# A two-layer encoder kernel: the sums of hT placed after the second pair of heads, and the last pair's norm run beside the last dilated head

## The chip, the cores and the metric

The kernel runs on one core of a Trainium2 chip. The metric is the device time in microseconds (us) of one execution, the median of the runs shown.

## The reference

Two layers of a hybrid encoder on 512 positions of width 1024, everything in float32, and a last RMSNorm. A layer normalises its input, makes all projections with one matrix `w_in`, runs three kinds of attention on them, gates and merges them, and adds an output projection to the input. Cut to what the change is near:

```python
def mixer_layer(x, mem, layer_idx, g_norm, w_in, lam_p, w_mem_kv, g_mem, ...):
    h = rmsnorm(x, g_norm)
    z = jnp.einsum('bsd,dn->bsn', h, w_in)
    dq, dk, dv, dg, lq, lk, lv, lg, mq, mg, mgate = jnp.split(z, splits, axis=-1)
    ...
    o_a = diff_attention(dq, dk, dv, lam, rel_bias[:, :8])      # 8 heads, two softmax maps each
    o_a = rmsnorm(o_a) * (1.0 - lam_init)                       # over the 128 values of a head
    y_a = (o_a * silu(dg)) @ w_br_diff
    ...                                                         # 3 x 4 dilated window heads -> y_b
    ...                                                         # 4 memory heads -> y_m
    gates = jax.nn.sigmoid(mgate).reshape(B, S, 3, D_MODEL)
    merged = gates[:, :, 0] * y_a + gates[:, :, 1] * y_b + gates[:, :, 2] * y_m
    return x + merged @ w_out
```

## The kernel before

**Precision and engines.** Each float32 product is made of three matmuls on halves: a value is split into a rounded `hi` and a rest `lo` (`split`: ACT writes `hi` with a copy, DVE writes `lo` as the difference; L106 and L107), and `mm3` (L214 to L217) issues hi·hi, hi·lo and lo·hi. PE is TensorE, DVE VectorE, ACT ScalarE, POOL GpSimd, SP the engine whose queue issues most DMAs.

**Weights.** They come in one fixed order. SP issues the loads into `w_raw` (three buffers), ACT makes `w_hi` (four buffers) and DVE `w_lo` (three), two weights ahead of the projection that uses them. A projection to feature-major form (`proj_fm`) is 24 matmuls into one of four PSUM buffers with the tag "mm"; `b_ps` and `f_ms`, below, use the same four.

**One layer.** `hT_hi` and `hT_lo` hold the normalised input, transposed. At the start of layer 0 the memory keys and values, the memory queries (`m_qh`, `m_ql`) and the table of relative biases (`bias_tables`: three matmuls `b_ps` and copies `b_t` on DVE, L350 and L352, behind one done ahead) are made. Then come four steps j = 0 to 3, each with one pair of differential heads and one dilated head. `weave` runs generators by turns, so that their code is issued mixed: first `dil_proj(j)` with `diff_att(j)`, then `diff_proj(j+1)` with `dil_att(j)`. In `diff_att` each head makes scores `f_s`, a DVE operation that adds the bias and finds the row minimum (`tensor_tensor_reduce`, L532; its result is `f_e`), an Exp on ACT, the weighted difference of the two maps on DVE, PE transposes (`wT_ps`), their split (`f_wThi`, `f_wTlo`), and the products with the values into `f_o`, which ACT copies to `f_osb`. `dil_att` is alike, with scores `d_s` and exponentials `d_e`. `diff_norm(j)` follows at the end of each step: for each of the two heads a Square on ACT (`f_sq`), its split (`f_sqh`, `f_sql`), two matmuls with ones (`f_ms`), an Identity on ACT, a reciprocal on DVE (L569), and two stores (`u_d`, `v_d`).

**The sums of hT.** Late in the layer, in `merge`, pairs of gate projections are made with fewer products, by sums of quarters of hT. `right_sums` (L256 to L282) makes them as `t_sum`: for each of two halves ten DVE operations and four stores to `t_d`, with four buffers. Its generator is woven into step j = 1. `merge` loads them back with POOL's DMAs (`t_in`).

**What sets the order.** The program is recorded in the order of the code, but the order on each engine is set by a scheduler, which may issue an instruction earlier where its operands and buffers allow; `tc.issue_after(x)` keeps what is recorded under it from being placed ahead of instruction x. Within an engine, and within SP's queue, instructions then run in that order, and one that waits holds all behind it.

Of the kernel before, what the change touches and what calls it, by code (L numbers as in the profile page):

```python
# [9 lines left out]
F32 = mybir.dt.float32  # L10
# [3 lines left out]
ALU = mybir.AluOpType  # L14
# [40 lines left out]
def encoder_kernel(ctx: ExitStack, tc: tile.TileContext, x, mem, g_norm, w_in, diff_lambda,  # L55
# [196 lines left out]
        add(c12, prod(3, 0, b22), c12)  # L252

    H0, H1 = slice(0, 256), slice(256, 512)

    def right_sums(pool):  # L256

        def acc(out, x, y, op):
            nc.vector.tensor_tensor(out=out, in0=x, in1=y, op=op)

        for k2 in range(2):
            def quarter(kh, ts):
                ks = slice(4 * kh + 2 * k2, 4 * kh + 2 * k2 + 2)
                return f32(hT_hi[:, ks, ts]), f32(hT_lo[:, ks, ts])

            b11, b12, b21, b22 = quarter(0, H0), quarter(0, H1), quarter(1, H0), quarter(1, H1)
            t1, t2, t3, t4 = [pool.tile([128, 2, 256], F32, tag="ts", name="t_sum", bufs=4) for _ in range(4)]
            for t, x, y in ((t1, b12, b11), (t3, b22, b12)):
                acc(t, x[0], y[0], ALU.subtract)
                yield  # L270
                acc(t, t, x[1], ALU.add)
                yield
                acc(t, t, y[1], ALU.subtract)
                yield
            for t, x, y in ((t2, b22, t1), (t4, b21, t2)):
                acc(t, x[0], y, ALU.subtract)
                yield
                acc(t, t, x[1], ALU.add)
                yield
            for i, t in enumerate((t1, t2, t3, t4)):  # L280
                dma(t_d[i, k2], t)
            yield  # L282
# [41 lines left out]

    def bias_tables(pool):

        lh = pool.tile([105, 96], F32, tag="tmp", name="b_lh", bufs=3)[:, 0:4 * N_BIAS]
        for i in range(3):
            for r in range(4):
                pdma(lh[35 * i:35 * i + 32, r * N_BIAS:(r + 1) * N_BIAS], rel_bias)  # L330
# [178 lines left out]
    def diff_att(l, j, P, proj, lam):  # L509
        Q, K, vhi, vlo = proj  # L510
        O = []
        for s in range(2):
# [5 lines left out]
            for half in range(2):  # L518
                whi = P["ae"].tile([128, 4, 256], F32R, tag="x4", name="f_wThi", bufs=4)
                wlo = P["ae"].tile([128, 4, 256], F32R, tag="x4", name="f_wTlo", bufs=4)  # L520
                for c2 in range(2):
# [4 lines left out]
                    for m in range(2):  # L526
# [2 lines left out]
                        nc.tensor.matmul(sp, lhsT=qh[:, cs], rhs=K[s, m], start=True, stop=False)  # L529
                        nc.tensor.matmul(sp, lhsT=ql[:, cs], rhs=K[s, m], start=False, stop=True)  # L530
                        em = P["al"].tile([128, S], F32, tag="e", name="f_e", bufs=4)
                        nc.vector.tensor_tensor_reduce(  # L532
                            out=em.rearrange("p (c b) -> p c b", c=4), in0=sp, in1=bt[:, 3 - c:7 - c],
                            op0=ALU.add, op1=ALU.min, scale=-1.0, scalar=3e38, accum_out=stt[:, m:m + 1])
                        nc.scalar.activation(em, em, AF.Exp, scale=-1.0, bias=stt[:, m:m + 1],  # L535
                                             accum_out=stt[:, 2 + m:3 + m])
                        e.append(em)
# [18 lines left out]

    def diff_norm(j, P, O):

        for s, o in enumerate(O):
            tmp = lambda name, dt=F32: P["al"].tile([128, S], dt, tag="tmp", name=name, bufs=3)  # L560
            sq, sqh, sql = tmp("f_sq"), tmp("f_sqh", F32R), tmp("f_sql", F32R)
            nc.scalar.activation(sq, o, AF.Square)
            split(sqh, sql, sq)
            ms = mm([128, S], name="f_ms")
            nc.tensor.matmul(ms, lhsT=ones, rhs=sqh, start=True, stop=False)
            nc.tensor.matmul(ms, lhsT=ones, rhs=sql, start=False, stop=True)
            dma(u_d[2 * j + s], o)
            nc.scalar.activation(sq, ms, AF.Identity, bias=eps_t, scale=1.0 / 128)
            nc.vector.reciprocal(sq, sq)  # L569
            dma(v_d[2 * j + s], sq)  # L570


    def qk_split(ae, o, scale, n0):
# [247 lines left out]
    for l in range(DEPTH):  # L821
# [48 lines left out]
        for j in range(4):  # L870
            dp, O = weave((dil_proj(l, j, P), 10), (diff_att(l, j, P, fp, lam), 8))
            if j < 3:
                gens = [(diff_proj(l, j + 1, P), 8), (dil_att(l, j, P, dp), 4)]
                if j == 1:
                    gens.append((right_sums(al), 22))
                fp = weave(*gens)[0]
            else:
                weave((dil_att(l, j, P, dp), 4))
            diff_norm(j, P, O)
        close(al_c)  # L880
        close(ae_c)
        yu_c, yu = opened(f"yu{l}", "left")
# [86 lines left out]
```

## Time and profile before

| | before |
|---|---|
| median of three runs | 1755.63 us (1754.11 to 1756.03) |
| profiled execution | 1754.84 us |
| its span | 1753.1 us |
| mean granted clock of TensorE in it | 0.997 of 2.4 GHz |
| PE busy | 1724.0 us (98%) |
| DVE, ACT, POOL busy | 1152.4, 888.9, 174.0 us |

The span runs from the first to the last instruction in the profile; 1.7 us of the time lie around it. A share of busy time is over the whole span; where an engine stands idle is read from windows and from the waits. "PE mm L215 <- DVE b_t L352" means that a matmul on line 215 into `mm` stood for the instruction that writes `b_t` on line 352, or for what that one set free.

### The profile page before, as it was taken

The numbers are of one execution on the slowest core, as the hardware profiler recorded it, in microseconds if no ns is written. First come the engines' busy times: TensorE is split into PE (matmuls) and PEld (weight loads), VectorE is DVE, ScalarE is ACT, GpSimd is POOL, SyncE is SP. The second block draws the span as 40 slices with busy tenths as digits, with TensorE's granted clock in tenths as the row PEclk, the third lists the DMA queues.
The fourth block names the chain that finished last, engine by engine and source line by source line (L and its number), as shares of the span: only waits on it lengthen the run. The fifth ranks groups of instructions, "written<-read, shape, count | busy, mean of one in ns | idle before, by whom it ended". The sixth has DMA issues, their size and how long they took to land.

```text
span 1753.1 us, 25712 instructions
## 1 busy us (share of the span) xinstructions
PE 1724.0 (98%) x9732; PEld 1515.8 (86%) x9732; DVE 1152.4 (66%) x1963; ACT 888.9 (51%) x1516; POOL 174.0 (10%) x141
## 2 busy tenths in 40 slices
PE   7899999999999999999999999999999999999998
PEld 6698889889898889998888998898988888889986
DVE  6766575666766586676476756667657647766663
ACT  6355555545545573343354655455455548533433
POOL 2200000000000033341000000000000100344200
PEclk9999999999999999999999999999999999999999
DMA  9752243332443643332663333324323438333242
GB/s 266 170 135 84 77 119 96 93 89 83 114 132 98 204 145 98 102 108 82 203 190 110 108 95 94 88 82 114 102 78 105 136 90 251 105 97 109 85 151 78
DMA packets 313084, 208.80 MB, mean 119 GB/s; under 512 B 15268, under 2 KB 284580, under 8 KB 312960
## 3 DMA queue, kind: packets, MB, share of 16 engines
q1 hardware_dynamic: 309648, 199.28, 39.0%
q0 software_dynamic: 3312, 7.88, 1.9%
q8 instruction: 76, 1.25, 0.3%
q14 instruction: 48, 0.39, 0.1%
HBM read 182.08 MB, written 25.02 MB: 118 GB/s over the span
## 4 chain that ended last, share of the span: by engine, by line
PE 95%; DMA 2%; DVE 1%; ACT 1%; issue 1%; SPq 0%; ACTq 0%; DVEq 0%
PE mm L215 23%; PE mm L217 23%; PE mm L216 23%; PE s_mm L217 4%; PE s_mm L215 4%; PE s_mm L216 4%; PE wT_ps L506 2%; PE f_s L529 2%; PE f_s L530 2%; DMA w_raw<-in_w_mem_kv 1%; PE f_o L216 1%; PE f_o L215 1%; PE f_o L217 1%; PE d_o L655 1%; PE d_s L631 1%
## 5 line engine op out<-in xcount | busy, mean ns | idle before, releaser
L107 DVE TENSOR_TENSOR w_lo<-w_raw,w_hi 128x1024 fp32r<-128x1024 f32 (+2 forms) x256 | 304.7, 1191 | 218.9 <-PE mm L217 171.6
L106 ACT ACTIVATE w_hi<-w_raw 128x1024 fp32r<-128x1024 f32 (+2 forms) x256 | 250.8, 980 | 389.2 <-PE mm L216 197.4
L215 PE MATMUL mm<-hT_hi,w_hi 128*128 128x512 f32 x1024 | 405.7, 397 | 5.1 <-DVE b_t L352 2.8
L217 PE MATMUL mm<-hT_hi,w_lo 128*128 128x512 f32 x1024 | 403.0, 394 | 0.0
L216 PE MATMUL mm<-hT_lo,w_hi 128*128 128x512 f32 x1024 | 403.0, 394 | 0.0
L215 PEld LDWEIGHTS mm<-hT_hi,w_hi 128*128 128x128 f32 x1024 | 193.2, 189 | 45.6 <-DVE b_t L352 4.5
L217 PEld LDWEIGHTS mm<-hT_hi,w_lo 128*128 128x128 f32 x1024 | 193.0, 188 | 39.9
L216 PEld LDWEIGHTS mm<-hT_lo,w_hi 128*128 128x128 f32 x1024 | 193.4, 189 | 38.1 <-DVE hT_lo L107 0.2
L217 PE MATMUL mm<-w_hi,hT_lo 128*128 128x384 f32 (+2 forms) x640 | 210.0, 330 | 0.0
L215 PE MATMUL mm<-w_hi,hT_hi 128*128 128x384 f32 (+2 forms) x640 | 209.6, 328 | 0.0
L216 PE MATMUL mm<-w_lo,hT_hi 128*128 128x384 f32 (+2 forms) x640 | 208.2, 326 | 0.0
L106 ACT ACTIVATE w_hi<-s_raw 128x1024 fp32r<-128x1024 f32 x80 | 76.1, 952 | 168.7 <-PE mm L216 105.1
L215 PEld LDWEIGHTS mm<-w_hi,hT_hi 128*128 128x128 f32 x640 | 120.9, 189 | 6.0
L216 PEld LDWEIGHTS mm<-w_lo,hT_hi 128*128 128x128 f32 x640 | 120.8, 189 | 6.1
L217 PEld LDWEIGHTS mm<-w_hi,hT_lo 128*128 128x128 f32 x640 | 120.7, 189 | 5.1
L107 DVE TENSOR_TENSOR w_lo<-s_raw,w_hi 128x1024 fp32r<-128x1024 f32 x80 | 99.1, 1239 | 32.8 <-issue 32.8
L535 ACT ACTIVATE f_e<-f_e,f_st 128x512 f32<-128x512 f32 x128 | 92.0, 721 | 49.7 <-DVE f_st L532 49.7
L294 POOL DMA_DIRECT2D t_in<-t_d x16 | 8.9, 562 | 1013.1 <-PE f_o L217 582.2
L215 PE MATMUL mm<-u_hi,w_hi 128*128 128x512 f32 x256 | 101.2, 395 | 0.0
L216 PE MATMUL mm<-u_lo,w_hi 128*128 128x512 f32 x256 | 101.2, 395 | 0.0
L217 PE MATMUL mm<-u_hi,w_lo 128*128 128x512 f32 x256 | 101.1, 395 | 0.0
L532 DVE CUSTOM_DVE_ANT_0 f_e<-f_s,f_bias 128x512 f32<-128x512 f32 x128 | 84.4, 682 | 6.8 <-PE f_s L530 6.7
(248 smaller groups left out, 3365.4 us busy)
## 6 DMA issues: line engine op xcount, KB each, us to landing
w_raw<-in_w_in SPq DMA_DIRECT2D x128, 512.0 KB, 4.0
s_raw<-in_w_in SPq DMA_DIRECT2D x80, 256.0 KB, 3.1
w_raw<-in_w_in SPq DMA_DIRECT2D x96, 128.0 KB, 2.4
w_raw<-in_w_mem_kv SPq DMA_DIRECT2D x16, 512.0 KB, 5.9
w_raw<-in_w_in SPq DMA_DIRECT2D x32, 256.0 KB, 2.9
u_raw<-u_d SPq DMA_DIRECT2D x32, 256.0 KB, 4.8
w_raw<-in_w_br_diff SPq DMA_DIRECT2D x16, 512.0 KB, 4.1
w_raw<-in_w_out SPq DMA_DIRECT2D x16, 512.0 KB, 3.8
```

Of the source, the lines that this page charges most:

```text
L106: nc.scalar.activation(hi, src, AF.Copy)
L107: nc.vector.tensor_tensor(out=lo, in0=src, in1=f32(hi), op=ALU.subtract)
L215: nc.tensor.matmul(o, lhsT=lh, rhs=rh, start=start, stop=False)
L216: nc.tensor.matmul(o, lhsT=lh, rhs=rl, start=False, stop=False)
L217: nc.tensor.matmul(o, lhsT=ll, rhs=rh, start=False, stop=stop)
L506: nc.tensor.transpose(t[:, i], s, ident)
L529: nc.tensor.matmul(sp, lhsT=qh[:, cs], rhs=K[s, m], start=True, stop=False)
L530: nc.tensor.matmul(sp, lhsT=ql[:, cs], rhs=K[s, m], start=False, stop=True)
L532: nc.vector.tensor_tensor_reduce(out=em.rearrange("p (c b) -> p c b", c=4), in0=sp, in1=bt[:, 3 - c:7 - c], op0=ALU.add, op1=ALU.min, scal ...
L535: nc.scalar.activation(em, em, AF.Exp, scale=-1.0, bias=stt[:, m:m + 1], accum_out=stt[:, 2 + m:3 + m])
L631: nc.tensor.matmul(sp2[:, g - 1], lhsT=Q[g][:, cs], rhs=K[g][:, cs], start=True, stop=True)
L655: nc.tensor.matmul(oh[:, qs], lhsT=v23[:, c, (g - 1) * 128:g * 128], rhs=w23[:, g - 1, qs], start=False, stop=c2 == 1 and g == 2)
```

## The change

The list `mark` keeps the latest `tensor_tensor_reduce` of `diff_att`. The DVE operations of `right_sums` are recorded under `issue_after` of that instruction; as the generator runs after the second pair's `diff_att`, it is the last reduce of that pair. `diff_norm` becomes a generator in two parts: first Square, split and the store of `u_d` for both heads, then, head by head, the matmuls, the Identity, the reciprocal and the store of `v_d`. For j < 3 it is run to its end in the place where it stood; for j = 3 it is woven with `dil_att`. Its temporary buffers are six instead of three.

```diff
@@ -252,11 +252,13 @@
         add(c12, prod(3, 0, b22), c12)
 
     H0, H1 = slice(0, 256), slice(256, 512)
+    mark = []
 
     def right_sums(pool):
 
         def acc(out, x, y, op):
-            nc.vector.tensor_tensor(out=out, in0=x, in1=y, op=op)
+            with tc.issue_after(mark[0].ins):
+                nc.vector.tensor_tensor(out=out, in0=x, in1=y, op=op)
 
         for k2 in range(2):
             def quarter(kh, ts):
@@ -324,7 +326,7 @@
 
     def bias_tables(pool):
 
-        lh = pool.tile([105, 96], F32, tag="tmp", name="b_lh", bufs=3)[:, 0:4 * N_BIAS]
+        lh = pool.tile([105, 96], F32, tag="tmp", name="b_lh", bufs=6)[:, 0:4 * N_BIAS]
         for i in range(3):
             for r in range(4):
                 pdma(lh[35 * i:35 * i + 32, r * N_BIAS:(r + 1) * N_BIAS], rel_bias)
@@ -529,9 +531,9 @@
                         nc.tensor.matmul(sp, lhsT=qh[:, cs], rhs=K[s, m], start=True, stop=False)
                         nc.tensor.matmul(sp, lhsT=ql[:, cs], rhs=K[s, m], start=False, stop=True)
                         em = P["al"].tile([128, S], F32, tag="e", name="f_e", bufs=4)
-                        nc.vector.tensor_tensor_reduce(
+                        mark[:] = [nc.vector.tensor_tensor_reduce(
                             out=em.rearrange("p (c b) -> p c b", c=4), in0=sp, in1=bt[:, 3 - c:7 - c],
-                            op0=ALU.add, op1=ALU.min, scale=-1.0, scalar=3e38, accum_out=stt[:, m:m + 1])
+                            op0=ALU.add, op1=ALU.min, scale=-1.0, scalar=3e38, accum_out=stt[:, m:m + 1])]
                         nc.scalar.activation(em, em, AF.Exp, scale=-1.0, bias=stt[:, m:m + 1],
                                              accum_out=stt[:, 2 + m:3 + m])
                         e.append(em)
@@ -556,18 +558,23 @@
 
     def diff_norm(j, P, O):
 
+        parts = []
         for s, o in enumerate(O):
-            tmp = lambda name, dt=F32: P["al"].tile([128, S], dt, tag="tmp", name=name, bufs=3)
+            tmp = lambda name, dt=F32: P["al"].tile([128, S], dt, tag="tmp", name=name, bufs=6)
             sq, sqh, sql = tmp("f_sq"), tmp("f_sqh", F32R), tmp("f_sql", F32R)
             nc.scalar.activation(sq, o, AF.Square)
             split(sqh, sql, sq)
+            dma(u_d[2 * j + s], o)
+            parts.append((sq, sqh, sql))
+        yield
+        for s, (sq, sqh, sql) in enumerate(parts):
             ms = mm([128, S], name="f_ms")
             nc.tensor.matmul(ms, lhsT=ones, rhs=sqh, start=True, stop=False)
             nc.tensor.matmul(ms, lhsT=ones, rhs=sql, start=False, stop=True)
-            dma(u_d[2 * j + s], o)
             nc.scalar.activation(sq, ms, AF.Identity, bias=eps_t, scale=1.0 / 128)
             nc.vector.reciprocal(sq, sq)
             dma(v_d[2 * j + s], sq)
+            yield
 
 
     def qk_split(ae, o, scale, n0):
@@ -874,9 +881,10 @@
                 if j == 1:
                     gens.append((right_sums(al), 22))
                 fp = weave(*gens)[0]
+                for _ in diff_norm(j, P, O):
+                    pass
             else:
-                weave((dil_att(l, j, P, dp), 4))
-            diff_norm(j, P, O)
+                weave((dil_att(l, j, P, dp), 4), (diff_norm(j, P, O), 4))
         close(al_c)
         close(ae_c)
         yu_c, yu = opened(f"yu{l}", "left")
```

The lines below are those that the scheduled programs have. Numbers behind a name tell one buffer or tile from another; line numbers shift by up to 7 in the changed kernel.

**DVE at the start of layer 0**, around the last copies of the bias tables, before the change (`w_lo` are weights' low halves, `m_ql` those of the memory queries):

```order
L259 TENSOR_TENSOR t_sum_3280<-t_sum_3280,hT_lo_89 128x512
L107 TENSOR_TENSOR w_lo_555<-w_raw_552,w_hi_554 128x1024
L259 TENSOR_TENSOR t_sum_3282<-t_sum_3282,hT_lo_89 128x512
L580 SCALAR_TENSOR_TENSOR m_ql_549<-mm_523,m_qh_548 128x512
L259 TENSOR_TENSOR t_sum_3280<-t_sum_3280,hT_lo_89 128x512
L107 TENSOR_TENSOR w_lo_590<-w_raw_587,w_hi_589 128x1024
L259 TENSOR_TENSOR t_sum_3282<-t_sum_3282,hT_lo_89 128x512
L580 SCALAR_TENSOR_TENSOR m_ql_584<-mm_558,m_qh_583 128x512
L259 TENSOR_TENSOR t_sum_3281<-hT_hi_88,t_sum_3280 128x512
L259 TENSOR_TENSOR t_sum_3281<-t_sum_3281,hT_lo_89 128x512
L107 TENSOR_TENSOR w_lo_737<-w_raw_734,w_hi_736 128x1024
L352 COPY b_t_661<-b_ps_659 80x512
```

and after it:

```order
L354 COPY b_t_653<-b_ps_651 80x512
L107 TENSOR_TENSOR w_lo_555<-w_raw_552,w_hi_554 128x1024
L587 SCALAR_TENSOR_TENSOR m_ql_549<-mm_523,m_qh_548 128x512
L107 TENSOR_TENSOR w_lo_590<-w_raw_587,w_hi_589 128x1024
L587 SCALAR_TENSOR_TENSOR m_ql_584<-mm_558,m_qh_583 128x512
L107 TENSOR_TENSOR w_lo_737<-w_raw_734,w_hi_736 128x1024
L354 COPY b_t_661<-b_ps_659 80x512
L354 COPY b_t_673<-b_ps_671 80x512
L354 COPY b_t_681<-b_ps_679 80x249
```

The `t_sum` operations are gone from here; `b_t_661` comes right behind `w_lo_737` in both.

**DVE at the end of the second pair of heads in layer 0**, before the change:

```order
L538 RECIPROCAL f_st_2880<-f_st_2880 128x2
L539 TENSOR_TENSOR f_st_2880<-f_st_2880,lam_707 128x1
L540 TENSOR_SCALAR f_e_2890<-f_e_2890,f_st_2880 128x512
L541 SCALAR_TENSOR_TENSOR f_e_2884<-f_e_2884,f_st_2880,f_e_2890 128x512
L107 TENSOR_TENSOR f_wTlo_2823<-wT_ps_2841,f_wThi_2822 128x4x128
L107 TENSOR_TENSOR w_lo_2951<-w_raw_2948,w_hi_2950 128x1024
L107 TENSOR_TENSOR d_vlo_2784<-mm_2786,d_vhi_2783 128x128
L107 TENSOR_TENSOR d_vlo_2784<-mm_2787,d_vhi_2783 128x128
L107 TENSOR_TENSOR d_vlo_2784<-mm_2788,d_vhi_2783 128x128
```

and after it:

```order
L261 TENSOR_TENSOR t_sum_3033<-t_sum_3033,hT_lo_89 128x512
L540 RECIPROCAL f_st_2880<-f_st_2880 128x2
L261 TENSOR_TENSOR t_sum_3035<-t_sum_3035,hT_lo_89 128x512
L261 TENSOR_TENSOR t_sum_3033<-t_sum_3033,hT_lo_89 128x512
L541 TENSOR_TENSOR f_st_2880<-f_st_2880,lam_707 128x1
L261 TENSOR_TENSOR t_sum_3035<-t_sum_3035,hT_lo_89 128x512
L107 TENSOR_TENSOR f_wTlo_2823<-wT_ps_2841,f_wThi_2822 128x4x128
L261 TENSOR_TENSOR t_sum_3034<-hT_hi_88,t_sum_3033 128x512
L542 TENSOR_SCALAR f_e_2890<-f_e_2890,f_st_2880 128x512
L107 TENSOR_TENSOR w_lo_2951<-w_raw_2948,w_hi_2950 128x1024
L261 TENSOR_TENSOR t_sum_3034<-t_sum_3034,hT_lo_89 128x512
L543 SCALAR_TENSOR_TENSOR f_e_2884<-f_e_2884,f_st_2880,f_e_2890 128x512
```

The `t_sum` operations now stand between the steps of the last softmax difference (`f_st`, `f_e`) and ahead of the split `f_wTlo`; the later ones follow behind these rows, mixed with the `d_vlo` splits.

**PE at the last pair of heads in layer 0**, from the last product of the second head, before the change:

```order
L217 MATMUL f_o_4899<-f_wThi_5036,f_vlo_4388 128x256
L215 MATMUL d_s1_5249<-d_kh_4654,d_qh_4725 128x512
L216 MATMUL d_s1_5249<-d_kl_4655,d_qh_4725 128x512
L217 MATMUL d_s1_5249<-d_kh_4654,d_ql_4726 128x512
L565 MATMUL f_ms_5379<-f_sqh_5374,ones_82 128x512
L215 MATMUL mm_5410<-hT_hi_88,w_hi_5134 128x512
```

and after it:

```order
L217 MATMUL f_o_4899<-f_wThi_5036,f_vlo_4388 128x256
L215 MATMUL d_s1_5269<-d_kh_4654,d_qh_4725 128x512
L216 MATMUL d_s1_5269<-d_kl_4655,d_qh_4725 128x512
L217 MATMUL d_s1_5269<-d_kh_4654,d_ql_4726 128x512
L638 MATMUL d_s2_5273<-d_k_4786,d_q_4857 128x128
L638 MATMUL d_s2_5273<-d_k_4892,d_q_4959 128x128
L572 MATMUL f_ms_5308<-f_sqh_5212,ones_82 128x512
L215 MATMUL mm_5410<-hT_hi_88,w_hi_5134 128x512
```

Two score matmuls `d_s2` moved ahead of the matmul of the norm, which keeps its place behind `f_o` and `d_s1`.

**ACT at the same place**, before the change:

```order
L568 ACTIVATE f_sq_5360<-f_ms_5366,eps_t_84 128x512
L605 ACTIVATE d_v23_4999<-mm_5003 128x256
L552 ACTIVATE f_osb_5130<-f_o_4899 128x512
L562 ACTIVATE f_sq_5373<-f_osb_5130 128x512
L106 ACTIVATE f_sqh_5374<-f_sq_5373 128x512
L638 ACTIVATE d_e_5223,d_st_5222<-d_e_5223,d_st_5222 128x768
```

and after it:

```order
L574 ACTIVATE f_sq_5204<-f_ms_5261,eps_t_84 128x512
L612 ACTIVATE d_v23_4999<-mm_5003 128x256
L645 ACTIVATE d_e_5237,d_st_5236<-d_e_5237,d_st_5236 128x768
L554 ACTIVATE f_osb_5130<-f_o_4899 128x512
L565 ACTIVATE f_sq_5211<-f_osb_5130 128x512
L106 ACTIVATE f_sqh_5212<-f_sq_5211 128x512
L645 ACTIVATE d_e_5268,d_st_5267<-d_e_5268,d_st_5267 128x768
```

An Exp (`d_e`) moved ahead of the copy `f_osb` of the second head's result.

## Rows read from the trace of the kernel before

**Rows 1.** the busy table of the page: busy time of each engine, its share of the span, instructions.

```profile
PE 1724.0 (98%) x9732; PEld 1515.8 (86%) x9732; DVE 1152.4 (66%) x1963; ACT 888.9 (51%) x1516; POOL 174.0 (10%) x141
```

**Rows 2.** windows of the span: from:to in us, length, busy us of PE, PEld, DVE, ACT and POOL with their instructions, mean granted TensorE clock (1.00 is 2.4 GHz, 0.50 is 1.2 GHz), DMA share, GB/s.

```profile
50.00:75.00 25.00, 20.97 (x91) 17.00 (x90) 18.85 (x29) 7.76 (x15) 5.37 (x10) 0.92 0.67 166
70.00:75.00 5.00, 3.71 (x10) 2.96 (x11) 5.00 (x9) 2.85 (x9) 3.01 (x6) 0.66 0.91 234
275.00:300.00 25.00, 25.00 (x148) 23.71 (x148) 16.91 (x38) 13.40 (x28) 0.00 (x0) 1.00 0.40 109
300.00:325.00 25.00, 25.00 (x130) 21.51 (x129) 13.43 (x28) 13.25 (x26) 0.00 (x0) 1.00 0.17 53
525.00:550.00 25.00, 23.65 (x124) 20.04 (x123) 18.25 (x29) 15.03 (x28) 0.00 (x0) 1.00 0.38 122
905.00:935.00 30.00, 30.00 (x138) 24.79 (x137) 26.33 (x39) 14.47 (x21) 0.00 (x0) 1.00 0.71 218
1375.00:1400.00 25.00, 23.33 (x133) 20.77 (x133) 15.58 (x30) 11.75 (x23) 4.57 (x8) 1.00 0.53 166
```

**Rows 3.** waits of PE over the whole span: what waited, for what, us in total, times, longest.

```profile
PE mm L215 <- DVE b_t L352: 2.8, 1, 2.8
PE f_ms L565 <- ACT f_sqh L106: 2.6, 2, 1.3
...
PE b_ps L350 <- DVE m_ql L580: 1.2, 1, 1.2
PE f_ms L566 <- DVE f_sql L107: 0.3, 1, 0.3
```

**Rows 4.** timeline of PE, layer 0, 59 to 79 us: start, length, engine, line, operation, out<-in, tile, count, and in brackets the idle time before it and what ended it. From the first row to the second are 23 matmuls, from the fourth to the fifth 24.

```profile
59.76 0.39 PE L216 MATMUL mm<-hT_lo,w_hi 128*128 128x512 f32 x1
...
64.97 0.38 PE L350 MATMUL b_ps<-b_oh,b_parts 105*80 105x512 bf16 x1
...
68.23 0.27 PE L350 MATMUL b_ps<-b_oh,b_parts 105*80 105x249 bf16 x1 [1.24 <-DVE m_ql L580]
71.29 0.80 PE L215 MATMUL mm<-hT_hi,w_hi 128*128 128x512 f32 x1 [2.79 <-DVE b_t L352]
...
78.42 0.39 PE L215 MATMUL mm<-hT_hi,w_hi 128*128 128x512 f32 x1
```

**Rows 5.** timeline of DVE in the same stretch, same columns.

```profile
60.41 0.69 DVE L259 TENSOR_TENSOR t_sum<-hT_hi 128x512 f32<-128x512 f32 x1 [6.05 <-DMA t_d<-t_sum]
61.02 0.68 DVE L259 TENSOR_TENSOR t_sum<-t_sum,hT_lo 128x512 f32<-128x512 f32 x1
...
62.82 1.22 DVE L107 TENSOR_TENSOR w_lo<-w_raw,w_hi 128x1024 fp32r<-128x1024 f32 x1
...
70.56 1.28 DVE L352 COPY b_t<-b_ps 80x512 f32<-80x512 f32 x2
```

**Rows 6.** timeline of SP's queue (first row) and of ACT (second row) in the same stretch.

```profile
51.73 10.32 SPq L281 DMA_DIRECT2D t_d<-t_sum  x4
...
68.15 1.06 ACT L106 ACTIVATE w_hi<-w_raw 128x1024 fp32r<-128x1024 f32 x1 [6.83 <-DMA w_raw<-in_w_in]
```

**Rows 7.** all instructions that write or read the tile `t_sum`: line, engine, operation, count, ns as min/median/max, first and last start; the last row is the time of its stores `t_d<-t_sum` from issue to landing.

```profile
L259 DVE TENSOR_TENSOR t_sum<-t_sum,hT_lo x24: 674/683/693, 49.8 to 930.2; 128x512 f32<-128x512 f32 x24
...
DMA to landing us min/median/max: 2.0/4.3/8.7
```

**Rows 8.** timelines at the last pair of heads: ACT in layer 0 (three rows), PE in layer 0 (one), then PE and DVE in layer 1.

```profile
532.20 0.60 ACT L552 ACTIVATE f_osb<-f_o 128x512 f32<-128x512 f32 x1 [0.70 <-PE f_o L217]
...
533.49 0.63 ACT L106 ACTIVATE f_sqh<-f_sq 128x512 fp32r<-128x512 f32 x1
534.96 0.94 ACT L638 ACTIVATE d_e<-d_e,d_st 128x768 f32<-128x768 f32 x1 [0.83 <-DVE d_st L635]
...
534.18 0.50 PE L565 MATMUL f_ms<-f_sqh,ones 128*128 128x512 f32 x1 [1.32 <-ACT f_sqh L106]
...
1399.69 0.51 PE L566 MATMUL f_ms<-f_sql,ones 128*128 128x512 f32 x1 [0.32 <-DVE f_sql L107]
...
1398.94 0.69 DVE L107 TENSOR_TENSOR f_sql<-f_sq,f_sqh 128x512 fp32r<-128x512 f32 x1 [4.24 <-DMA v_d<-f_sq]
```

**Rows 9.** timelines at the second pair of heads, layer 0: DVE (first row), PE (the rest).

```profile
304.17 0.68 DVE L107 TENSOR_TENSOR f_wTlo<-wT_ps,f_wThi 128x512 fp32r<-128x512 f32 x1
...
302.04 0.60 PE L506 MATMUL wT_ps<-ident,f_e 128*128 128x128 f32 x4
...
304.05 0.48 PE L215 MATMUL mm<-hT_hi,w_hi 128*128 128x512 f32 x1
...
309.08 0.28 PE L216 MATMUL f_o<-f_wTlo,f_vhi 128*128 128x256 f32 x1
```

**Rows 10.** timelines at the first pair of heads, layer 0: DVE (two rows), PE (last row).

```profile
238.00 3.35 DVE L569 RECIPROCAL f_sq<-f_sq 128x512 f32<-128x512 f32 x1
...
242.86 0.73 DVE L541 SCALAR_TENSOR_TENSOR f_e<-f_e,f_st 128x512 f32<-128x512 f32 x1
...
248.49 0.49 PE L506 MATMUL wT_ps<-ident,f_e 128*128 128x128 f32 x3
```


## The prediction, on record before the changed kernel was run

> **What bounds the kernel now.** I read the busy table first, then the windows, then PE's waits, then single instructions. PE is busy 1724.0 of 1753.1 us [rows 1], so 29.1 us is everything a pure reordering can win from its idle time; the work itself is unchanged by the diff (the same matmuls, the same vector passes). The windows say where those 29 us lie. Some 22 us lie at the start and end, where the change moves nothing. Three places are left that it touches: 50 to 75 us, where 25.00 − 20.97 = 4.03 us are idle and the granted clock is 0.92; 525 to 550 us, 1.35 us idle; 1375 to 1400 us, 1.67 us idle [rows 2]. PE's waits give each a name [rows 3]: 2.8 us for the bias tables' copy `b_t` and 1.2 us for `m_ql` (the first place), twice 1.3 us for ACT's `f_sqh` and 0.3 us for DVE's `f_sql` (the other two: the norm of the last two heads, once a layer).
>
> **First place: why PE waits for a DVE copy.** The mixing of work there is seen on DVE [rows 5]: a `t_sum` stood 6.05 us for a store `t_d<-t_sum`, and everything behind it on DVE waited with it. On SP four such stores sit from 51.73 to 62.05, because each waits for its sum, and the weight loads behind them on that queue come late too: ACT's `w_hi` waited 6.83 us for `w_raw` and began at 68.15 [rows 6]. `w_lo` of that weight and behind it the two copies `b_t` (70.56, in program order after it) are what PE's next projection waits for: its PSUM buffer is held by the first `b_ps`. So PE stands 1.24 us at 68.23 and 2.79 us before 71.29, in sum 4.03 [rows 4].
>
> The wait has a second price. After it the windows show a granted clock of 0.66 in 70 to 75 us [rows 2], so part of that stretch ran at 1.2 GHz instead of 2.4. The next projection's 24 matmuls took 78.42 − 71.29 = 7.13 us; at the pace before the stall, (64.97 − 59.76)/23 = 0.2265 us each, they take 5.44 [rows 4]. The clock cost 1.69 us. Whole price of the place: 5.7 us.
>
> **What the change does to it.** The twenty `t_sum` operations of a layer can't start before the last reduce of the second pair of heads, so in layer 0 they leave this stretch of DVE altogether, and their eight stores leave SP's queue. What follows on DVE in the new order is `w_lo`, `m_ql`, `w_lo`, `m_ql`, then `w_lo_737`, then `b_t_661`. By hand, with the durations of before: the load for weight 737 is no longer behind a blocked store; `w_lo_737` then waits only for a weight buffer that PE gives back when the projection that ended at 64.97 is through, takes 1.22 us [rows 5] and ends at about 66.2; `b_t_661` adds 0.64 (half of the 1.28 of two copies [rows 5]): 66.8. PE finishes the memory scores at 68.23 − 1.24 = 66.99 and reaches the projection at about 67.1 with the third `b_ps` (0.27, [rows 4]) before it. The copy is there some 0.3 us ahead, so I expect no wait and no fall of the clock: −5.7 us. The margin is thin and makes a rival below.
>
> Here a page bears on the size. The Trainium skill, "TensorE: Matmul & The Clock Gate", section "What's actually happening", says that the number of slow matmuls after a restart changes from run to run of one kernel (6, 11, 14). This trace has one case only, 7 to 8 slow starts. By the page and the step of 0.43 instead of 0.23 us the clock's share could be an estimated 1.2 to 2.8 us rather than 1.69, and the saving 5.2 to 6.8.
>
> **Where the twenty sums go.** They stand behind the reduces of the second pair, in layer 0 from about 295 us, in layer 1 from about 1152. One takes 0.68 us [rows 7], 0.61 from start to start (60.41 to 61.02 [rows 5]), so 12 us are put into a stretch in which DVE has 25 − 16.91 = 8.1 us free in 275 to 300 and 11.6 free in 300 to 325 [rows 2]. Fourteen of them stand ahead of the `f_wTlo` that ran at 304.17 [rows 9]; walked through with the waits of before it ends at about 309.5 instead of 304.85. Who waits for it is PE's `f_o` matmul at 309.08 [rows 9], which in the new PE order stands behind the whole projection and part of the next: 42 matmuls after 304.05 at 0.2275, that is 313.7. The slack is about 4 us. Before that PE wants `f_e` for the transposes that ran at 302.04; the new DVE order gives it at about 302.2 and PE comes to them at 303.7: slack 1.5. In layer 1 the kernel before already had these sums elsewhere (907 to 931 us), with a `t_d` store among the weight loads in the same way, and PE was busy 30.00 of 30.00 us in 905 to 935 [rows 2]. I take nothing for the move. Its bounds: a gain is excluded, since PE has no idle time in 275 to 325; a loss has its price among the rivals.
>
> **The last pair.** The chain on ACT is `f_osb` at 532.20, then Square, then `f_sqh` at 533.49, and `f_ms` starts at 534.18: 1.98 us of three dependent ACT steps after `f_o`. PE had 0.66 us of `d_s` to put between, and stood for 1.32 [rows 8]. The new code is meant to mix the norm of both heads into the last dilated head, but the second head's sum of squares can't begin before its `f_o` is complete, and in the new order PE still has just `f_o`, three `d_s1`, now two `d_s2` (pulled ahead, about 0.3 us), then `f_ms`. On ACT an Exp of 0.94 us now stands ahead of `f_osb`, where in before it came after the chain [rows 8]; by hand the chain starts 0.15 us later in layer 0 and 0.3 later in layer 1. So the wait shrinks by the 0.3 of `d_s2` and grows by 0.15 to 0.3: I take −0.1 in the first and 0 in the second. The third wait, 0.32 us at 1399.69, is another matter: `f_sql` there stood 4.24 us for a store of `f_sq`, that is for one of three temporary buffers [rows 8]. With six it has no such wait: −0.3. Nothing is left of it below 0, and no more than 0.32 to win. Sum for the last pairs: −0.4, bounds 0 and −3.0 (all of [rows 3]).
>
> For the other three pairs of a layer both heads' squares come first and then both reciprocals follow one another: two of 3.35 us in a row on DVE instead of 12 us apart. Behind them at the first pair of layer 0 is the `f_e` that ran at 242.86; it would end at about 248.8, and PE's transposes of it, at 248.49 in before [rows 10], now stand behind more matmuls, at about 253. Slack 4: nothing. The six places are alike.
>
> **Sum.** −5.7 − 0.4 = −6.1 against the profiled 1754.84, that is 1748.8. The median of the runs shown is 0.79 above the profiled execution, so on that scale 1749.6, or −0.34%.
>
> **Rivals.**
> - *The last pairs' waits vanish as well.* For: they are what half of the diff is about. Against: the order of PE above. It would save another 2.6 − 0.1 = 2.5 us from 1749.6: 1747.1.
> - *The gap at the bias tables closes only half.* The margin was 0.3 us; one late weight (DMA share is 0.67 in 50 to 75 [rows 2]) puts `b_t` behind `w_lo_737` past PE's arrival. With 2 of 4.03 us left and the clock's 1.69 lost all the same, A gives −2.0 in place of −5.7: 1753.3; with half the clock's price 1752.5.
> - *The last pairs' stalls grow until the clock falls.* Exp ahead of `f_osb` is the cause, about 1.0 us more wait in each, and then the 1.69 of the first place twice: +5.4, 1755. Against: a granted clock of 1.00 around stalls of 1.32 in before [rows 2], and a shift by hand of only 0.15 to 0.3. The Trainium skill, same page, section "HAM oscillation — how this bites in real kernels", tells of a kernel that falls back to the slow clock at every long wait between groups of matmuls; by it each of these stalls would be priced with the clock once it is long enough. The trace has no fall at them so far.
> - *Slower: DVE blocks at the second pair.* The first four stores `t_d` stand on SP at about 297 to 300 us, and the fifth sum's buffer is free only when the first has landed. The landings took 2.0 to 8.7 us, median 4.3 [rows 7]; the walk needs the first by 303.2, about 6 us after its issue, and has 4 to 4.6 us of slack behind. A landing of over 10.5 us makes PE wait; 13.6 us make 3.1 us of wait and 1.69 of clock, 4.8 us in each layer, 9.6 in both, which is where the total passes +0.2% (6.1 saved, 3.5 over): 1759.1. Against: DMA is at 0.40 and 0.17 there, against 0.67 where the 8.7 was seen [rows 2]. The Trainium skill, "DMA: Bandwidth & Descriptors", section "Latency and other measured facts", has the fixed cost of a DMA grow with the load on the memory, which agrees; no run here has a landing near 10 us.
>
> **Chances.** Forecast 0.62 (own range 1748 to 1751.5), waits vanish 0.10, half a gap 0.14, falling clock 0.09, blocked at the second pair 0.05. A measurement of this kernel can tell about 0.2% from no change, that is 3.5 us: below 1752.1 is faster, above 1759.1 slower. Faster: 0.62 + 0.10 and a few hundredths of the half-closed gap and of the small end of the falling clock, 0.76. Slower: 0.05. Same: 0.19. The range takes in the vanished waits below, less the 0.8 between profiled execution and median, and the half-closed gap above, with as much: 1746.3 to 1754.0; it leaves out the last two rivals.
>
> **What would show it.** Right: no PE wait for `b_t` or `m_ql`, granted clock near 1.00 in 50 to 75, no DVE wait for `t_d` there; two PE waits of 1.1 to 1.4 for `f_sqh` still; no wait of `f_sql` for a store; PE idle 0 in 275 to 325 and 1130 to 1185. Wrong: a PE wait for `f_wTlo`, `f_e` or `w_lo` at the second pair, a granted clock below 1.00 after 1390 or 532, or a DVE wait for `t_d<-t_sum` of more than 4 us. The forecast fails most easily at the 0.3 us of margin for `b_t_661`.

## The result, and the profile after

| | before | after |
|---|---|---|
| median | 1755.83 us (1754.11 to 1757.22, 4 executions) | 1745.87 us (1745.23 to 1747.22, 4 executions) |
| ratio | | 0.9945, 95% interval 0.9933 to 0.9957 |
| the same again, on another chip | 1755.20 (16 executions) | 1745.65 (5 executions), 0.9943, interval 0.9929 to 0.9957 |
| span of the profiled execution | 1753.1 | 1745.5, and 1744.1 in the second |

The change takes 9.6 to 10.0 us off, 0.55%. The forecast was 1749.6 (its own sum, 1755.63 − 6.1, gives 1749.5), with a range from 1746.3: the direction was right, the size was not, and the time lies 0.4 us below the range.

The waits of TensorE in the changed kernel, those over 1 us and one other (columns as in [rows 3]):

```profile
PE mT_ps L391 <- DVE mem_h L382: 10.7, 2, 9.0
PE mm L215 <- ACT hT_hi L106: 3.1, 1, 3.1
PE f_ms L572 <- ACT f_sqh L106: 2.7, 2, 1.3
PE mT_ps L391 <- ACT mT_keep L393: 1.5, 1, 1.5
PE mm L215 <- DVE gate L308: 0.3, 1, 0.3
```

The waits for `b_t` and `m_ql` (2.8 and 1.2 us) and the one for `f_sql` (0.3) are gone; the two for `f_sqh` are as they were. The windows that answer to [rows 2]:

```profile
50.00:75.00 25.00, 25.00 (x114) 20.58 (x114) 11.94 (x24) 9.46 (x19) 7.91 (x14) 0.97 0.55 116
70.00:75.00 5.00, 5.00 (x24) 4.14 (x23) 3.87 (x14) 3.29 (x12) 4.48 (x9) 1.00 0.86 150
275.00:300.00 25.00, 25.00 (x155) 24.34 (x155) 21.97 (x47) 14.76 (x31) 0.00 (x0) 1.00 0.47 136
300.00:325.00 25.00, 25.00 (x122) 20.89 (x121) 19.40 (x38) 12.27 (x24) 0.00 (x0) 1.00 0.35 115
525.00:550.00 25.00, 23.67 (x115) 19.70 (x115) 17.35 (x25) 14.36 (x22) 0.00 (x0) 1.00 0.31 95
1375.00:1400.00 25.00, 23.67 (x126) 20.62 (x125) 18.27 (x27) 14.90 (x26) 4.29 (x8) 1.00 0.54 179
```

In 50 to 75 us TensorE is busy throughout; the granted clock of 0.97 stems from the first 1.5 us, behind the wait for `hT_hi`. The twelve microseconds of `t_sum` appear on DVE in 275 to 325 (21.97 and 19.40 us busy instead of 16.91 and 13.43, 11.0 us more), and TensorE stays at 25.00 of 25.00.

**The first place, measured.** TensorE's rows there, to be set beside [rows 4]: the last projection ends where `b_ps` starts, and the next one has made its 24 matmuls at the last row.

```profile
66.17 0.60 PE L352 MATMUL b_ps<-b_oh,b_parts 105*80 105x512 bf16 x2
...
68.03 0.28 PE L217 MATMUL m_s<-mk_hi,m_ql 128*128 128x256 f32 x1
68.25 0.50 PE L215 MATMUL mm<-hT_hi,w_hi 128*128 128x512 f32 x1
...
73.82 0.39 PE L215 MATMUL mm<-hT_hi,w_hi 128*128 128x512 f32 x1
```

Before, this took 78.42 − 64.97 = 13.45 us, now 73.82 − 66.17 = 7.65: 5.8 us less, where the prediction had 5.7. That term was right to 0.1 us. DVE's rows show how near it was; the last line is the view of the tile `b_t`, with the length of its copies in ns (min/median/max):

```profile
66.37 1.23 DVE L107 TENSOR_TENSOR w_lo<-w_raw,w_hi 128x1024 fp32r<-128x1024 f32 x1 [3.12 <-PE mm L217]
67.51 1.60 DVE L354 COPY b_t<-b_ps 80x512 f32<-80x512 f32 x3
...
L354 DVE COPY b_t<-b_ps x4: 402/677/689, 49.9 to 68.7; 80x512 f32<-80x512 f32 x3, 80x249 f32<-80x249 f32 x1
```

The copy that frees the PSUM buffer is the first of the three and ended at 67.51 + 0.68 = 68.19; TensorE's next projection started at 68.25, 0.06 us behind it. Before, where it plainly waited for this copy, it started as closely behind it (70.56 + 0.68 = 71.24, then 71.29). And the step from 68.03 to 68.25 is 0.22 us, where a matmul of 256 columns has 0.12 (below). So TensorE still waited for the copy, some 0.1 us, too short to be listed: there was no margin. 5.8 of 9.6 to 10.0 us are found. The rest, some 4 us, is for the most part in stretches where the page shows TensorE busy all the time.

### The profile page after: what moved, and what is told of

The parts are those of the page before. It is cut to its first block, busy times and chain, and to the rows that moved or that the text cites. A ratio compares the mean times of both kernels' runs of the same rounds, so it can differ in the third digit from the quotient of the medians.

```text
span 1745.5 us, 25691 instructions
## 1 busy us (share of the span) xinstructions
PE 1719.6 (99%) x9732; PEld 1515.9 (87%) x9732; DVE 1152.6 (66%) x1963; ACT 888.4 (51%) x1516; POOL 174.6 (10%) x141
## 4 chain that ended last, share of the span: by engine, by line
PE 97%; DMA 1%; SPq 1%; ACT 1%; DVE 0%; issue 0%; ACTq 0%
PE mm L215 23%; PE mm L216 23%; PE mm L217 23%; PE s_mm L217 4%; PE s_mm L215 4%; PE s_mm L216 4%; PE wT_ps L508 2%; PE f_s L532 2%; PE f_s L531 2%; PE f_o L215 1%; PE d_o L662 1%; PE f_o L217 1%; PE f_o L216 1%; PE d_s L638 1%; PE d_o L216 0%; PE d_o L217 0%
```

## The experiments

All times are device times against the kernel before on the same chip.

**One part alone.** The first kernel has `mark` and `issue_after` alone:

```diff
+            with tc.issue_after(mark[0].ins):
-            nc.vector.tensor_tensor(out=out, in0=x, in1=y, op=op)
+                nc.vector.tensor_tensor(out=out, in0=x, in1=y, op=op)
```

> The sums of hT tied behind the second pair's last reduce; the norm is as before, with three temporary buffers. Theory 1 (the wait at the bias tables and its slow matmuls are the larger part; a smaller part is the number of changes on TensorE between one-pass matmuls and plain float32 ones, about 0.1 us each): no wait for b_t or m_ql, the clock near 1.00 in 50 to 75 us, which is -5.9 us; the order has 435 such changes against 443, which is -0.8; the two waits of 1.3 us for f_sqh and the 0.3 us wait for f_sql stay. In sum -6.7 us, a ratio of 0.996. Rival W (weaving the last pair earns the rest): the same -5.9, ratio 0.9966, nothing from the changes. Rival N (what lies beyond -5.9 in the changed kernel is scatter of the executions): -5.9.

Measured: 1750.48 us against 1755.53, ratio 0.9973, interval 0.9963 to 0.9984: −5.05. The waits for `b_t` and `m_ql` are gone, and a new one is there: one line of TensorE's waits, then two of those of its weight loads (PEld):

```profile
PE d_o L215 <- ACT d_wThi L106: 0.6, 2, 0.3
```

```profile
PEld f_s L531 <- DVE f_st L534: 2.0, 6, 0.4
PEld d_o L215 <- ACT d_wThi L106: 1.5, 2, 0.7
```

At the second pair of each layer a `d_o` matmul waits for ACT. So the sums do have a price at that place when they are moved alone. In the changed kernel that wait is not there, so the parts need not add up.

The second kernel has the generator, six buffers and the woven last pair, without `mark`. The third is the second without the weaving:

```diff
-                weave((dil_att(l, j, P, dp), 4), (diff_norm(j, P, O), 4))
+                weave((dil_att(l, j, P, dp), 4))
+                for _ in diff_norm(j, P, O):
+                    pass
```

The fourth is the kernel before with one number changed, in two places that share the tag:

```diff
-            tmp = lambda name, dt=F32: P["al"].tile([128, S], dt, tag="tmp", name=name, bufs=3)
+            tmp = lambda name, dt=F32: P["al"].tile([128, S], dt, tag="tmp", name=name, bufs=6)
```

> The norm as a generator, six temporary buffers, the last pair woven; the sums of hT as before. Theory 1: the wait at the bias tables stays (4.0 us and the slow matmuls behind it); the order has 427 changes between one-pass and plain float32 matmuls against 443, which is -1.6 us, and the wait of f_sql for a store goes, -0.3; the two waits for f_sqh stay at 1.2 to 1.4. In sum -1.9 us, ratio 0.9989. Rival W: -2 to -3 us too, but from the last pairs: a smaller wait for f_sqh. Rival N: within 0.3 us of before, ratio 0.9998.

> As the run before in the list, but the last pair's norm is issued behind the last dilated head instead of woven into it; six buffers. Theory 1: the same 427 changes, so -1.9 us as with the weaving, ratio 0.9989. Rival W: the gain of the weaving is gone, 0 to -0.3 us, ratio 0.9999. Rival N: as before within 0.3 us.

> The kernel before with six instead of three temporary buffers of the norm, nothing else. Theory 1: the scheduler already moves the second head's squares up and sets the four norm matmuls side by side (427 changes against 443), so the whole -1.9 us of the norm's part come with the buffers alone, ratio 0.9989. Rival W: nothing but the wait of f_sql, -0.3 us. Rival N: -0.3 us at most.

Measured: 1753.29, 1752.50 and 1753.18 us against 1755.53 (ratios 0.9987, 0.9981, 0.9988, each interval clear of 1 and 0.0017 wide): −2.2, −3.0 and −2.4. The three are one program: their instructions stand in the same order on TensorE, DVE, ScalarE and SP, names aside, so the spread between them is that of the measurement. The generator and the weaving, the larger part of the diff, move nothing. Six temporary buffers alone let the scheduler make the second head's squares early and set the four `f_ms` matmuls side by side. The same holds with the sums moved: as scheduled, `mark` and six buffers alone give the changed kernel's order on these engines (this one was not run). Rival W (the weaving earns the rest) and rival N (it is scatter) are out.

**What do the buffers buy? The first answer was wrong.** Matmuls on split halves are called one-pass here; the transposes and some small products are on plain float32. The four `f_ms` matmuls side by side reduce the changes between the two kinds in the order from 443 to 427, and to 423 with the sums moved, and theory 1 gave each a price of 0.1 us. Two kernels test it. Each adds 64 matmuls of 128 columns to the changed kernel, whose results are overwritten; they differ in the place alone. The first puts it ahead of a score matmul of its kind:

```diff
+                        if m == 1:
+                            nc.tensor.matmul(sp[:, 0], lhsT=qh[:, cs], rhs=K[s, m][:, 0:128], start=True, stop=True)
```

The second puts it between the second and the third transpose:

```diff
+            if i == 2 and extra:
+                nc.tensor.matmul(t[:, i], lhsT=extra[0], rhs=extra[1], start=True, stop=True)
```

> The changed kernel once more, on the same chip and beside the same runs of the kernel before as the next ones. If the two parts of the change add up as they were measured apart (-5.1 and -2.2 us), -7.3 us, ratio 0.9958. If the -10 us of the first measurement hold, the parts help each other by 2.7 us: the order has 423 changes between one-pass and plain float32 matmuls with both parts, 435 and 427 with one of them.

> The changed kernel with one more matmul of 128 columns for each of the 64 softmax blocks of the differential heads, put right ahead of the second score matmul and of the same one-pass kind (its result is overwritten): 64 matmuls more, the same 423 changes of kind. Theory 1 and every rival: 64 x (0.06 to 0.12) = 4 to 8 us more than the changed kernel, so 1750 to 1754. It is the base for the next run.

> The same 64 extra matmuls, but each put between the second and the third of the four plain float32 transposes of that block: 547 changes of kind instead of 423. Theory 1 (a change of kind costs TensorE time that no wait shows): more than the run before by 62 x 0.09 = 5.6 us, if only the return to one-pass costs, to 124 x 0.1 = 12 us, if both do. Rival (changes of kind cost nothing, the smooth drift of the changed kernel against the one before has another cause): within 1 us of the run before.

Measured: the changed kernel again 1745.65 us, 9.55 below before. The parts measured apart make −7.3 to −8.1, so they seem to help each other; more on this below. With the extra matmul among its kind: 1751.84 (0.9983, interval 0.9974 to 0.9992); between the transposes: 1749.66 (0.9969, 0.9957 to 0.9981). The kernel with 124 changes more is 2.2 us the shorter one, where theory 1 wanted it 5.6 to 12 us longer. Theory 1 falls: a change of kind has no price near 0.1 us. What the rows show is the price of a long matmul behind a short one (the extra matmul among its kind, the extra one between the transposes, and a group of transposes without one):

```profile
124.07 0.22 PE L532 MATMUL f_s<-f_k,f_qh 128*128 128x128 f32 x1
124.13 0.45 PE L533 MATMUL f_s<-f_k,f_qh 128*128 128x512 f32 x1
124.41 0.39 PE L534 MATMUL f_s<-f_k,f_ql 128*128 128x512 f32 x1
```

```profile
134.69 0.38 PE L510 MATMUL wT_ps<-ident,f_e 128*128 128x128 f32 x2
134.82 0.31 PE L509 MATMUL wT_ps<-f_k,f_qh 128*128 128x128 f32 x1
134.97 0.41 PE L510 MATMUL wT_ps<-ident,f_e 128*128 128x128 f32 x2
135.13 0.48 PE L215 MATMUL mm<-hT_hi,w_hi 128*128 128x512 f32 x1
135.45 0.39 PE L216 MATMUL mm<-hT_lo,w_hi 128*128 128x512 f32 x1
```

```profile
127.22 0.60 PE L508 MATMUL wT_ps<-ident,f_e 128*128 128x128 f32 x4
127.57 0.48 PE L217 MATMUL mm<-hT_hi,w_lo 128*128 128x512 f32 x1
127.89 0.40 PE L215 MATMUL mm<-hT_hi,w_hi 128*128 128x512 f32 x1
```

In the first (extra matmul among its kind) the 512-column matmul behind it takes 124.41 − 124.13 = 0.28 us instead of 0.23. In the second the step after the transposes takes 0.32, as it does without the extra matmul, which joined a short group that was there already; the group takes 0.44 instead of 0.35. By these rows an extra matmul costs 0.11 us in the first kernel and 0.09 in the second; measured were 0.10 and 0.06, so a part of the 2.2 us stays open.

**The second answer: waits that TensorE's own rows hide.** Going by steps from start to start, not by idle time, the kernel before shows this at the first pair of layer 0 (TensorE and its weight loads; the last two rows are the undisturbed step of 256 columns):

```profile
235.70 0.28 PE L215 MATMUL d_o<-d_wThi,d_vhi 128*128 128x256 f32 x1
235.99 0.19 PEld L529 LDWEIGHTS f_s<-f_k,f_qh 128*128 128x128 f32 x1 [0.32 <-DVE f_st L532]
235.99 0.50 PE L529 MATMUL f_s<-f_k,f_qh 128*128 128x512 f32 x1
...
236.32 0.40 PE L530 MATMUL f_s<-f_k,f_ql 128*128 128x512 f32 x1
236.65 0.20 PEld L644 LDWEIGHTS w_ps<-ident,d_e 128*128 128x128 f32 x2 [0.37 <-issue]
236.68 0.41 PE L644 MATMUL w_ps<-ident,d_e 128*128 128x128 f32 x2
...
237.05 0.28 PE L217 MATMUL d_o<-d_wThi,d_vlo 128*128 128x256 f32 x1
237.17 0.28 PE L215 MATMUL d_o<-d_wThi,d_vhi 128*128 128x256 f32 x1
```

A 256-column matmul has 0.12 us to the next start when nothing waits, a 512-column one 0.23. Here the steps are 0.29, 0.33 and 0.36: 0.17, 0.10 and 0.13 us are lost, 0.40 in all. The score matmul `f_s` waits for a PSUM buffer that DVE has not read yet, because it stands only three matmuls behind the scores before it; `f_s` has two buffers, and no run gave it a third, so this cause rests on the rows. No PE row has a bracket, since a row is drawn 0.28 or 0.39 us long where the next one can start after 0.12 or 0.23; a wait shorter than that overlap leaves no idle time. The weight loads do have brackets. Their waits over the whole span before:

```profile
PEld w_ps L644 <- issue: 2.2, 6, 0.4
...
PEld f_s L529 <- DVE f_st L532: 1.9, 6, 0.3
PEld f_o L216 <- DVE f_wTlo L107: 0.7, 2, 0.4
PEld f_ms L566 <- DVE f_sql L107: 0.6, 1, 0.6
```

Six times (three pairs, two layers) 0.40 us is 2.4. The `f_o` at the last pairs loses 0.30 twice (its first two steps take 0.31 and 0.22 instead of 0.12): 0.6. The wait for `f_sql`, 0.32 in [rows 3], is 0.55 by start to start. In the changed kernel's second profile this list holds, for the whole attention, one line only:

```profile
PEld f_ms L572 <- ACT f_sqh L106: 3.0, 2, 1.5
```

and with six buffers alone the same four lines are gone (the list there has `b_t`, `hT_hi` and `f_sqh`, and none for `f_s`, `w_ps` or `f_o`). The place of the first pair now reads, in the changed kernel's first profile:

```profile
230.31 0.39 PE L532 MATMUL f_s<-f_k,f_ql 128*128 128x512 f32 x1
230.54 0.40 PE L572 MATMUL f_ms<-f_sqh,ones 128*128 128x512 f32 x1
230.78 0.39 PE L573 MATMUL f_ms<-f_sql,ones 128*128 128x512 f32 x1
231.01 0.39 PE L572 MATMUL f_ms<-f_sqh,ones 128*128 128x512 f32 x1
231.25 0.39 PE L573 MATMUL f_ms<-f_sql,ones 128*128 128x512 f32 x1
231.47 0.39 PE L215 MATMUL mm<-hT_hi,w_hi 128*128 128x512 f32 x1
```

Two more `f_ms` and a projection stand where `d_o` and the next scores stood, and every step is 0.22 to 0.24. Sum by rows: 5.8 + 2.4 + 0.6 + 0.55 = 9.35 us, against 9.55 and 9.96 measured. The sums alone keep the six waits of `f_s` (2.0 us of weight loads, above). The Trainium skill, "Perfetto Trace Analysis", section "Identifying the Most-Contended Engine", says that the busy share of matmuls is not a good measure of how close a kernel is to its roofline, because pipelined matmuls look smaller in the trace. This trace agrees on the measure, though here it is rows drawn longer than the step (0.39 against 0.23) that hide the waits: 3 us at a busy share of 100%.

By the same rows the buffers alone should give 2.4 + 0.6 + 0.55 = 3.55 us, and 2.2 to 3.0 were measured. The traces say where the rest is. All these kernels have the same first 400 matmuls, so the stretch from the start of the 401st to the start of the last can be set side by side (us, one profile each):

| | 401st starts | last starts | between | against before |
|---|---|---|---|---|
| before | 96.39 | 1745.37 | 1648.98 | |
| six buffers alone | 97.61 | 1743.27 | 1645.66 | −3.3 |
| generator and weaving | 98.29 | 1743.81 | 1645.52 | −3.5 |
| generator without weaving | 98.33 | 1743.88 | 1645.55 | −3.4 |
| sums alone | 90.14 | 1739.72 | 1649.58 | +0.6 |
| changed | 91.69 | 1737.77 | 1646.08 | −2.9 |
| changed, again | 90.77 | 1736.38 | 1645.61 | −3.4 |

Behind the first 96 us the buffers are worth 3.3 to 3.5 us, with the sums moved or not (the first profile of the changed kernel has a wait for `gate` besides, 0.8 us by its weight loads and 0.3 in the second), and the sums alone cost 0.6, the `d_o` wait. Matmul for matmul, that is, at points where both kernels have made the same ones, each of the six places gives 0.35 to 0.36 us with six buffers alone, and the last pairs 0.33 and 0.93. So the parts help each other by 0.6 us. What else seemed so lies in the first 96 us, where the three kernels with buffers alone came 1.2 to 1.9 us later than the kernel before: one had a wait for `hT_hi` of 3.8 us instead of 2.3, and in the other two the granted clock stayed low for longer behind `b_t` (0.66 in 70 to 80 us instead of 0.83). Why all three came out so is open.

**The waits that stayed.** Theory 2, that TensorE's waits are the whole matter, says that the two for `f_sqh` and the one for `hT_hi` are still to be had. In the first kernel ScalarE's high half of the fourth query weight is kept behind the high halves of hT, in the second the first gate's projection is written ahead of the last norm, whose first matmul is kept behind the twelfth of that projection, and the third has both (`last_hT` is the last of those halves, `part` runs the norm up to the first head's store, `after_k` is that twelfth matmul):

```diff
+            if key == ("in", 0, MQ + 384):
+                with tc.issue_after(last_hT[0].ins):
+                    nc.scalar.activation(hi, raw, AF.Copy)
...
+                weave((dil_att(l, j, P, dp), 4), (part(), 4))
+                first_gate[:] = [gate(l, U_COLS[U_ORDER[0]])]
+                for _ in dn:
+                    pass
...
+            with tc.issue_after(after_k[0].ins) if j == 3 and s else ExitStack():
+                nc.tensor.matmul(ms, lhsT=ones, rhs=sqh, start=True, stop=False)
```

> The changed kernel, with ScalarE's high half of the fourth memory query weight placed behind the last high halves of hT; in the kernels so far it stands ahead of them, waits for its load, and TensorE waits 2.3 to 3.8 us for hT at 47 us. Theory: that wait is decided by when a load lands in the busy first 50 us, and so is its part of the scatter between executions; without it the wait shrinks below 1.5 us and the execution gets 1.5 to 4 us shorter than the changed kernel (some of it the clock, where it fell). Rival (hT itself is late, the weight only stands in the idle time): no difference.

> The changed kernel, with the first gate's projection written ahead of the second head's norm of the last pair, and that norm's first matmul kept behind the twelfth matmul of the projection. Theory 2 (what moved the time is TensorE's waits, the long one at the bias tables and short ones that show only at its weight loads; the two waits of 1.3 us for f_sqh are still paid in full in the changed kernel): both waits go, -2.6 us against the changed kernel, some 1743.0. Rival (those waits lie beside work that is late anyway): no difference, 1745.6.

> The run before in this list together with hT's high halves ahead of the fourth query weight on ScalarE. Theory 2: the two gains are at different places and add up: -2.6 and -1.8 (measured alone) against the changed kernel, some 1741.2. Rival (one of them only moves the wait to the next weight): 1743 to 1744.

Measured: hT first 1743.81 (0.9940, interval 0.9927 to 0.9952), its wait at 1.1 us in the profile; norm later 1743.06 (0.9929, 0.9917 to 0.9942), both waits for `f_sqh` gone; both 1741.56 (0.9922, 0.9908 to 0.9935). Against the changed kernel's 1745.65 that is −1.8, −2.6 and −4.1, where −1.5 to −4, −2.6 and −4.4 were expected (the last two ran on another chip, where the kernel before took 1755.72 us instead of 1755.20). For `f_sqh` theory 2 holds. For `hT` less is shown. With the wait for the high half at 1.1 us the weight loads wait 1.4 us for the low half, a wait that the changed kernel has at 0.2 at most, and the granted clock in 45 to 55 us is 1.00 instead of 0.83. Executions at the same mean granted clock differ little: at 0.999 hT first took 1743.4 to 1743.8 us and the changed kernel 1743.9 (one execution), at 0.998 1745.6 and 1746.5 against 1745.1 to 1746.0. So, to go by the mean clock, most of the 1.8 us is that the clock fell once less in more of the executions (three of five at 0.999, where the changed kernel has one of five); that the edit caused this is not shown. The last kernel has the lowest median, 14 us below the kernel before, though its interval overlaps that of norm later. Its profile has no wait of TensorE behind the first 50 us, on the matmuls or on the weight loads.

**The place of the sums.**

```diff
-                if j == 1:
+                if j == 2:
                     gens.append((right_sums(al), 22))
```

> The changed kernel with the sums of hT tied behind the third pair of heads instead of the second. Theory 2: what counts is that they left the first 75 us; where DVE has slack the place is worth nothing, and the third pair has the same work as the second: 1745.0 to 1746.4. Rival (the place behind the second pair has its own price on DVE, 0.3 us per layer or more, as the sums alone showed at that place): 0.6 us or more off, on either side.

Measured: 1746.95 (0.9948, interval 0.9935 to 0.9962), with a profiled span of 1742.5, shorter than the changed kernel's. The median is 0.55 outside the band that theory 2 gave and its interval covers the changed kernel's; no difference is shown, and a price of 0.6 us in all at either place is not excluded.

## Why the prediction was off, by its own steps

- **The first place** (−5.7): right, 5.8 by start to start. Its cause, order and clock came as described; the margin of 0.3 us was not there, TensorE waited 0.1 us for the copy, and that no more was lost is partly luck: the rival of the half-closed gap was near.
- **Where the sums go** (0): right. The rows that answer to [rows 9] and [rows 7] are these, on DVE, TensorE and for the stores:

```profile
302.68 0.68 DVE L107 TENSOR_TENSOR f_wTlo<-wT_ps,f_wThi 128x512 fp32r<-128x512 f32 x1
```

```profile
308.79 0.28 PE L216 MATMUL f_o<-f_wTlo,f_vhi 128*128 128x256 f32 x1
```

```profile
DMA to landing us min/median/max: 2.0/2.3/3.3
```

  `f_wTlo` ended at 303.4 and TensorE used it at 308.8, a slack of 5.4 where 4 was worked out. The stores `t_d` landed in at most 3.3 us (8.7 before, where the DMA share was 0.67 and not 0.35 to 0.47), and DVE waited for none, so the slower rival had nothing to stand on. But the move alone costs a wait of `d_o`, seen with the sums alone, and that step did not see that it is the other part that takes this wait away.
- **"For the other three pairs of a layer … nothing"**: the step that failed. It asked only what could come late on DVE, because the prediction had set the idle 29.1 us as "everything a pure reordering can win from its idle time" and, for the second pair, taken 25.00 of 25.00 busy as proof that "a gain is excluded". The changed order removes six groups of short waits, 2.4 us by the rows and 2.1 matmul for matmul. The busy table of the changed kernel shows that busy time is no floor: that of the same 9732 matmuls is 4.4 us less (1724.0 before), by these waits and by the slow matmuls of the first place.

```profile
PE 1719.6 (99%) x9732; PEld 1515.9 (87%) x9732; DVE 1152.6 (66%) x1963; ACT 888.4 (51%) x1516; POOL 174.6 (10%) x141
```

- **The last pair** (−0.4): the 0.32 for `f_sql` went, and was worth 0.55; the waits for `f_sqh` stayed at 1.3, as said; the 0.6 of the `f_o` matmuls was missed for the same reason as above. So this term was about −1.1 by the rows, −1.3 matmul for matmul.
- **What the parts of the diff do**: the prediction followed the code's story (a generator, a weaving). The order of the program shows that the number of buffers does all of it. The step from the code's intention to the machine's order was not made edit by edit.
- The rivals with vanishing `f_sqh` waits, a falling clock at the last pairs, and a block at the second pair did not happen.

## What to carry to other kernels

A busy share of 100% on TensorE does not mean that nothing waits: measure the steps from start to start against the undisturbed step, or read the waits of the weight loads, before a term is set to zero. Before a microsecond or two is put down to an edit, compare executions at the same mean granted clock. When a change has several edits, look at the order that each produces alone; here one number did what thirty lines of code were written for. And two pairs of score matmuls in a row want other long work between them and the next pair, or, as the rows here read, the PSUM buffer's reader sets the pace.

## What was not expected of the hardware

Whether the clock falls behind the wait for `hT_hi` at 47 us varies between executions. In the window of 45 to 55 us it was 0.83 in seven profiles, with waits from 1.9 to 3.8 us (the changed kernel again 1.9, the kernel before 2.3, the changed kernel 3.1, six buffers alone 3.8), and 1.00 in three with 2.3, 2.7 and 3.3 us (the extra matmul among its kind, the one between the transposes, the sums alone) and in three with 1.1 to 1.4. So between 1.9 and 3.8 us the length of the wait does not decide it. The 0.83 means some eight matmuls at 1.2 GHz, 0.43 instead of 0.23 us each, so 1.6 us that one execution pays and another doesn't. The executions of one kernel show it too: with the extra matmul among its kind, five at a mean granted clock of 0.999 took 1750.9 to 1751.5 us and five at 0.997 or 0.998 took 1752.2 to 1754.7. It is part of the 2 to 4 us between the executions of one kernel. The kernel before has this fall besides the one at 71 us, so its trace has two cases, not the one that the prediction speaks of. The Trainium skill, "TensorE: Matmul & The Clock Gate", section "What's actually happening", has the number of slow matmuls change from run to run, and these windows agree: some eight, or none.
